# Block 1's neighbourhood attention: stacked Q, compact K, and P·V with V as the stationary operand

## The chip, the core and the metric

The kernel runs on one core of one Trainium2 chip. The metric is device microseconds (us) of one execution; lower is better. TensorE (PE) does matmuls and transposes, and the profile lists its weight loads apart (PEld); DVE, ACT and POOL are the vector, scalar and GpSimd engines, SP issues most DMAs. Each engine runs its own instructions in the order of the program.

## What is computed

Two transformer blocks follow each other on 512 tokens (plus 16 meta tokens in the first). The change lies in the first block's mixer: 8 heads of neighbourhood attention, head width 64, on an 8 x 64 grid. With 8 rows each query sees all 8 rows and 16 columns, plus the 16 meta keys; the meta queries attend to the meta keys alone. Then a root-mean-square norm over all 512 channels, with a gain.

```python
s_loc = jnp.einsum('bhrcd,bhrikd->bhrcik', qg, k_rows) + bias
s_loc = jnp.where(in_win[:, None, :], s_loc, -jnp.inf)
s_meta = jnp.einsum('bhrcd,bmhd->bhrcm', qg, km)
s_all = jnp.concatenate([s_loc.reshape(B, H, R, W, kh * W), s_meta], axis=-1)
p = jax.nn.softmax(s_all, axis=-1)
og = einsum('bhrcik,bhrikd->bhrcd', p_loc, v_rows) + einsum('bhrcm,bmhd->bhrcd', p_meta, vm)
...
o_na = rmsnorm(o_na, na_gain)
mix = jnp.concatenate([o_na, o_gl], axis=-1) @ w_o
```

Beside it the block has a gated linear attention (GLA, 4 heads, both directions), whose work is interleaved with the neighbourhood attention.

## The kernel before

Activations are held channel-major: 128 channels on the partitions, tokens along the row. A weight tile is split into a high and a low part (`wh`, `wl`, type fp32r) by ACT and DVE, so is the activation, and three products replace one (`gemm_outer`, L269 to L286). All projections of block 1 (`ps_w_in`, L284) go through it: each group of 128 output channels is 24 products of 272 tokens and 24 of 256, then a callback takes the result out of PSUM.

The neighbourhood attention goes by pairs of heads p = 0 to 3 (one 128-channel tile is two heads, e = 0, 1). For a pair, `cb_na` takes Q, K and V. Queries are cut into four column tiles `ct` of 16 columns x 8 rows = 128 queries; each sees 32 columns x 8 rows = 256 keys. Q is written into `QW` by column tile; K and V are written four times, once for each tile's 32 columns, by `window` (L551 to L560: eight DVE operations each for K and V), with the 16 meta keys behind (272 columns). V is then transposed (`pvw`, L588) to `VW`.

`na_pair` (L595) has, for each column tile and head (8 units a pair, 32 in all): one score product with 64 rows in type f32 (L615), a DVE operation that adds the mask and bias and finds the row's extreme (L620), the exponential with its sum on ACT (L621), a reciprocal (L622), three transposes of the probabilities (L623 to L625), copies out of PSUM (`pTs` on DVE, `pTm` on ACT), two P·V products with 128 keys and one with the 16 meta keys (L632, L634; the transposed probabilities are the stationary operand, 64 columns of V move), and an ACT copy scaled by the reciprocal (L635) to `ON`, token-major.

After the last pair, `ON` is squared and summed on ACT (L718), the root is taken (L719), each tile is scaled on DVE (L723), transposed back (`pnt`, L726) and split into `mixn`. Then comes `w_o`, whose first half of the products (`part(..., 1, ...)`, six groups of 12 products) needs only GLA's output `mixg`.

The order of the program is made by a scheduler from priorities: GLA first, then `na_pair` (low 1), then the projections (low 2), then `w_ple_2` (low 3) as filler at the end. A score tile takes one of three PSUM banks (`pn_`). Each engine keeps the order that was fixed at build time, whatever is ready.

Of the kernel before, what the change touches and what calls it, by code (L numbers as in the profile page):

```python
# [19 lines left out]
T = NM + S  # L20
# [62 lines left out]
def _pack_w(w, groups, kchunks, rows=None):  # L83
# [3 lines left out]
    for cols in groups:  # L87
# [10 lines left out]
        ("norm_ffn_2", 8), ("norm_ple_2", 8)]  # L98
# [58 lines left out]
class Ker:  # L157
# [130 lines left out]
    def rstd_fin(self, acc, n, pool, pp, name, r=None, rc=None):  # L288
# [14 lines left out]
        nc.scalar.activation(rc, ps[:bs, :nb], AF.Sqrt, bias=self.eps[:bs])  # L303
# [10 lines left out]
    def block1(self, emit):  # L314
# [77 lines left out]
        def cb_gla(gi, si, ps):  # L392
# [14 lines left out]
            elif gi in (3, 4):  # L407
                if si == 0:
                    cur["v"] = gl.tile([128, T], F32, tag="vT", name=f"vT{f}", bufs=2)
# [10 lines left out]
            else:  # L420
                if si == 0:
                    cur["v"] = gl.tile([128, T], F32, tag="vT", name=f"gT{f}", bufs=2)
# [10 lines left out]
        def gla(p):  # L433
# [22 lines left out]
            for d in range(2):  # L456
# [6 lines left out]
                E = gl.tile([128, T], F32, tag="E", name=f"E{p}{d}")  # L463
                iE = gl.tile([128, T], F32, tag="iE", name=f"iE{p}{d}")
# [7 lines left out]
                nc.vector.tensor_tensor(QS[d], qg[p], E, ALU.mult)  # L472
                nc.vector.tensor_tensor(KI[d], kg[p], iE, ALU.mult)
                nc.scalar.activation(DEC[:, d, 1:9], Ex[:, :, last], AF.Copy)
                nc.scalar.activation(DEC[:, d, 0:1], E[:, mlast:mlast + 1], AF.Copy)
                kx, ki = [t[d][:, 16:].rearrange("p (c t) -> p c t", t=64) for t in (KE, KI)]
# [72 lines left out]
        VM = [na.tile([16, 128], F32, name=f"VM{p}", bufs=1) for p in range(4)]  # L549

        def window(dst, ps, si, tagm):  # L551
            iv_ = ps[:, 16:272] if si == 0 else ps[:, 0:256]
            rv_ = rs[:, 16 + 256 * si:272 + 256 * si]
            for ct, w0 in enumerate((0, 8, 24, 32)):
                iv, rv = [t.rearrange("p (r c) -> p r c", c=64)[:, :, w0:w0 + 32] for t in (iv_, rv_)]
                ov = dst[:, ct, 128 * si:128 * si + 128].rearrange("p (r c) -> p r c", c=32)
                nc.vector.tensor_tensor(ov, iv, rv, ALU.mult)
            if si == 0:
                nc.vector.tensor_tensor(tagm, ps[:, 0:16], rs[:, :16], ALU.mult)
                nc.gpsimd.tensor_copy(dst[:, :, 256:272], tagm.rearrange("p (o k) -> p o k", o=1).to_broadcast([128, 4, 16]))  # L560

        def cb_na(gi, si, ps):
            p, j = (gi - 13) // 3, (gi - 13) % 3
            if j == 0:
                if si == 0:
                    cur["Q"] = na.tile([128, 4, 128], F32, tag="QW", name=f"QW{p}")
                    nc.vector.tensor_tensor(QM[:, p, :], ps[:, 0:16], rsq[:, :16], ALU.mult)
                iv = (ps[:, 16:272] if si == 0 else ps[:, 0:256]).rearrange("p (r t c) -> p r t c", r=4, t=4)
                rv = rsq[:, 16 + 256 * si:272 + 256 * si].rearrange("p (r t c) -> p r t c", r=4, t=4)
                base = cur["Q"][:, 0, 127 - 64 * si:128 - 64 * si]  # L570
                ov = bass.AP(base.tensor, base.offset, [list(base.ap[0]), [-16, 4], [128, 4], [-1, 16]])
                nc.vector.tensor_tensor(ov, iv, rv, ALU.mult)
            elif j == 1:
                if si == 0:
                    cur["K"] = na.tile([128, 4, 272], F32, tag="KW", name=f"KW{p}")
                window(cur["K"], ps, si, KM[:, p, :])
            else:
                if si == 0:
                    cur["V"] = na.tile([128, 4, 272], F32, tag="VTW", name=f"VTW{p}", bufs=1)
                    cur["vm"] = na.tile([128, 16], F32, tag="vtm", name=f"vtm{p}")  # L580
                window(cur["V"], ps, si, cur["vm"])
                if si == 1:
# [8 lines left out]
                    nc.tensor.transpose(pm[:16, :128], cur["vm"], ident)  # L591
                    nc.scalar.activation(VM[p], pm[:16, :128], AF.Copy)
                    cur[p] = (cur["Q"], cur["K"], VW)

        def na_pair(p):  # L595
            QW, KW, VW = cur[p]
            sm = na.tile([128, 2, 4], F32, tag="sm", name=f"sm{p}")
            bms = [[], []]
            for t, s in enumerate((15, 7, -1)):
                for e in range(2):  # L600
                    h = 2 * p + e
                    rt = na.tile([128, 256], F32, tag="rpb", name=f"rpb{h}{t}", bufs=2)
# [4 lines left out]
                    nc.gpsimd.tensor_tensor(bm[:, :256], nm[:, t, :256], rt, ALU.subtract)  # L607
                    nc.gpsimd.memset(bm[:, 256:], 0.0)
                    bms[e].append(bm)
            for ct in range(4):  # L610
                pzs = []
                for e in range(2):
                    rr = slice(64 * e, 64 * e + 64)
                    pz = pn_.tile([128, 512], F32, tag="n", name=f"pS{p}{ct}{e}")
                    nc.tensor.matmul(pz[:, :272], QW[rr, ct, :], KW[rr, ct, :], start=True, stop=True)  # L615
                    pzs.append(pz)
                for e, pz in enumerate(pzs):
                    s = na.tile([128, 272], F32, tag="s", name=f"s{p}{ct}{e}", bufs=3)
                    mx = na.tile([128, 1], F32, tag="mx", name=f"mx{p}{ct}{e}", bufs=4)
                    nc.vector.tensor_tensor_reduce(s, pz[:, :272], bms[e][(0, 1, 1, 2)[ct]], 1.0, 1e38, ALU.add, ALU.min, mx)  # L620
                    nc.scalar.activation(s, s, AF.Exp, bias=mx, scale=-1.0, accum_out=sm[:, e, ct:ct + 1])  # L621
                    nc.vector.reciprocal(sm[:, e, ct:ct + 1], sm[:, e, ct:ct + 1])  # L622
                    nc.tensor.transpose(pz[:, 0:128], s[:, 0:128], ident)  # L623
                    nc.tensor.transpose(pz[:, 128:256], s[:, 128:256], ident)
                    nc.tensor.transpose(pz[:16, 272:400], s[:, 256:272], ident)  # L625
                    pT = na.tile([128, 256], F32, tag="pT", name=f"pTs{p}{ct}{e}", bufs=2)
                    pTm = na.tile([16, 128], F32, tag="pTm", name=f"pTm{p}{ct}{e}", bufs=2)
                    nc.vector.tensor_copy(pT, pz[:, :256])
                    nc.scalar.activation(pTm, pz[:16, 272:400], AF.Copy)
# [56 lines left out]
        gr = na2.tile([128, 512], F32, name="na_gain")  # L686
        nc.sync.dma_start(gr, ins["na_gain"].to_broadcast([128, 512]))
# [18 lines left out]
        ptms = na2.tile([16, 8, 16], F32, name="ptms")  # L706
        nc.vector.tensor_copy(ptms, ptm[:16])
        pom = ps_.tile([128, 8, 64], F32, tag="s", name="pom")
        for h in range(8):
            nc.tensor.matmul(pom[:16, h, :], ptms[:, h, :], VM[h // 2][:, 64 * (h % 2):64 * (h % 2) + 64], start=True, stop=True)  # L710
        nc.vector.tensor_tensor(ONm.rearrange("p (h d) -> p h d", h=8), pom[:16], msum.to_broadcast([16, 8, 64]), ALU.mult)

        ss = na2.tile([128, 5], F32, name="nss")
        nc.vector.memset(ss, 1.0)
# [879 lines left out]
```

## Time and profile before

| | us |
|---|---|
| time, median of 3 runs | 1883.17 |
| lowest and highest run | 1872.4, 1884.64 |
| span of the profiled execution | 1873.3 |
| stretch from the first projection to `w_o` (27 to 335 us) in it | 308 |
| PE, DVE, ACT, POOL busy in that stretch | 301.8, 155.2, 132.4, 21.7 |

"Busy" of PE holds the drain of each product, so it overstates how full PE is; the chain of work that ended last, which gives the time from one step to the next, is the better measure. "PEclk" is the granted TensorE clock as a share of its higher level: 1.00 is 2.4 GHz, 0.50 is 1.2 GHz.

### The profile page before, as it was taken

What the parts mean: (1) busy time and instruction counts of PE and PEld (TensorE: products, weight loads), DVE (VectorE), ACT (ScalarE), POOL (GpSimd) and SP (SyncE); (2) the same over time, 40 slices, a digit from 0 to 9 for tenths busy, and PEclk for the clock granted to TensorE, in tenths of its full rate; (3) what the DMA queues carried; (4) which work ended last, traced back from release to release, by engine and by line L of the source; (5) the groups of instructions that cost most, each with busy time, mean ns of one, the idle gap of its engine ahead of it and who ended that gap; (6) DMA issues with size and microseconds to landing.
All of it is one profiled execution on the core that took longest, in us unless ns stands there. A gap on an engine that the chain in (4) does not pass through costs nothing.

```text
span 1873.3 us, 31022 instructions
## 1 busy us (share of the span) xinstructions
PE 1799.5 (96%) x11936; PEld 1506.6 (80%) x11936; DVE 1075.4 (57%) x2274; ACT 770.5 (41%) x1563; POOL 192.2 (10%) x217
## 2 busy tenths in 40 slices
PE   8999999989999999888789989999999999999998
PEld 7788888889998999866566768886678888888887
DVE  5644544787752677866746592437656553255445
ACT  6452434665442445653133432235434442234333
POOL 1000110110000001452211121112000000000000
PEclk9989989999999999998699997589999999999999
DMA  6111121653333334531221113112055333333334
GB/s 189 40 46 46 53 78 57 179 154 111 94 90 96 91 93 136 172 103 46 62 74 48 53 52 81 29 42 86 28 159 161 107 96 96 96 95 92 96 96 130
DMA packets 130789, 171.08 MB, mean 91 GB/s; under 512 B 44455, under 2 KB 59055, under 8 KB 130640
## 3 DMA queue, kind: packets, MB, share of 16 engines
q1 hardware_dynamic: 130640, 169.09, 31.1%
q8 instruction: 94, 1.54, 0.3%
q14 instruction: 55, 0.45, 0.1%
HBM read 155.42 MB, written 13.63 MB: 90 GB/s over the span
## 4 chain that ended last, share of the span: by engine, by line
PE 86%; DVE 7%; DMA 3%; issue 2%; ACT 2%; POOL 0%; SPq 0%; DVEq 0%; ACTq 0%; POOLq 0%
PE ps_w_ff L251 19%; PE ps_w_ffn_in L251 13%; PE ps_w_in L284 7%; PE ps_w_in L251 6%; PE ps_w_ffn_out L251 5%; PE ps_qkv L1277 3%; PE ps_w_out L251 2%; PE ps_w_ple_gate L251 2%; PE pP L1090 2%; PE ps_w_up_rwkv L251 1%; PE py L1214 1%; PE ps_w_up_attn L251 1%; PE ps_first L364 1%; PE paS L1350 1%; PE pS L632 1%
## 5 line engine op out<-in xcount | busy, mean ns | idle before, releaser
L203 DVE TENSOR_TENSOR wl_w_ff<-raw_w_ff,wh_w_ff 128x512 fp32r<-128x512 f32 x128 | 88.2, 689 | 131.6 <-ACT wh_w_ff L202 131.5
L202 ACT ACTIVATE wh_w_ff<-raw_w_ff 128x512 fp32r<-128x512 f32 x128 | 80.9, 632 | 194.7 <-PE ps_w_ff L251 185.9
L202 ACT ACTIVATE wh_w_in<-raw_w_in 128x512 fp32r<-128x512 f32 (+1 forms) x118 | 72.9, 623 | 101.9 <-PE ps_w_in L284 53.0
L203 POOL TENSOR_TENSOR wl_w_in<-raw_w_in,wh_w_in 128x512 fp32r<-128x512 f32 x60 | 82.0, 1371 | 254.6 <-ACT wh_w_in L202 192.2
L202 ACT ACTIVATE wh_w_ffn_in<-raw_w_ffn_in 128x512 fp32r<-128x512 f32 x96 | 60.1, 630 | 100.8 <-PE ps_w_ffn_in L251 87.4
L251 PE MATMUL ps_w_ff<-Yl,wh_w_ff 128*128 128x512 f32 x256 | 101.0, 395 | 0.0
L251 PE MATMUL ps_w_ff<-Yh,wh_w_ff 128*128 128x512 f32 x256 | 101.0, 395 | 0.0
L251 PE MATMUL ps_w_ff<-Yh,wl_w_ff 128*128 128x512 f32 x256 | 101.0, 395 | 0.0
L251 PE MATMUL ps_w_ffn_out<-Y_hi,wl_w_ffn_out 128*128 128x256 f32 (+1 forms) x256 | 83.5, 326 | 2.2 <-DVE wl_w_ffn_out L203 2.1
L251 PE MATMUL ps_w_ffn_out<-Y_hi,wh_w_ffn_out 128*128 128x256 f32 (+1 forms) x256 | 83.7, 327 | 0.0
L251 PE MATMUL ps_w_ffn_out<-Y_lo,wh_w_ffn_out 128*128 128x256 f32 (+1 forms) x256 | 83.5, 326 | 0.0
L251 PE MATMUL ps_w_ffn_in<-fa_hi,wl_w_ffn_in 128*128 128x258 f32 x352 | 73.9, 284 | 3.2 <-DVE wl_w_ffn_in L203 3.2
L203 DVE TENSOR_TENSOR wl_w_ffn_in<-raw_w_ffn_in,wh_w_ffn_in 128x512 fp32r<-128x512 f32 x96 | 65.8, 690 | 19.1 <-ACT wh_w_ffn_in L202 17.9
L251 PE MATMUL ps_w_ffn_in<-fa_hi,wh_w_ffn_in 128*128 128x258 f32 x352 | 73.8, 283 | 1.8 <-ACT wh_w_ffn_in L202 1.8
L203 DVE TENSOR_TENSOR wl_w_ffn_out<-raw_w_ffn_out,wh_w_ffn_out 128x512 fp32r<-128x512 f32 (+1 forms) x72 | 47.8, 669 | 47.7 <-ACT wh_w_ffn_out L202 47.5
L251 PE MATMUL ps_w_ffn_in<-fb_hi,wh_w_ffn_in 128*128 128x258 f32 x352 | 73.8, 284 | 0.0
L251 PE MATMUL ps_w_ffn_in<-fb_hi,wl_w_ffn_in 128*128 128x258 f32 x352 | 73.6, 283 | 0.2 <-DVE wl_w_ffn_in L203 0.2
L251 PE MATMUL ps_w_ffn_in<-fa_lo,wh_w_ffn_in 128*128 128x258 f32 x352 | 73.8, 283 | 0.0
L251 PE MATMUL ps_w_ffn_in<-fb_lo,wh_w_ffn_in 128*128 128x258 f32 x352 | 73.7, 283 | 0.0
L202 ACT ACTIVATE wh_w_ffn_out<-raw_w_ffn_out 128x512 fp32r<-128x512 f32 (+1 forms) x72 | 41.5, 582 | 62.4 <-PE ps_w_ffn_out L251 43.3
L251 PEld LDWEIGHTS ps_w_ffn_in<-fa_hi,wl_w_ffn_in 128*128 128x128 f32 x352 | 55.9, 190 | 3.6 <-DVE wl_w_ffn_in L203 3.6
L251 PEld LDWEIGHTS ps_w_ffn_in<-fa_hi,wh_w_ffn_in 128*128 128x128 f32 x352 | 55.8, 189 | 2.3 <-ACT wh_w_ffn_in L202 2.0
(645 smaller groups left out, 5274.4 us busy)
## 6 DMA issues: line engine op xcount, KB each, us to landing
raw_w_ff<-in_w_ff SPq DMA_DIRECT2D x128, 256.0 KB
raw_w_in<-in_w_in SPq DMA_DIRECT2D x116, 256.0 KB
raw_w_ffn_in<-in_w_ffn_in SPq DMA_DIRECT2D x96, 256.0 KB
raw_w_ffn_out<-in_w_ffn_out SPq DMA_DIRECT2D x40, 256.0 KB
raw_w_o<-in_w_o SPq DMA_DIRECT2D x32, 256.0 KB
raw_w_ffn_out<-in_w_ffn_out SPq DMA_DIRECT2D x32, 192.0 KB
gtd<-gt SPq DMA_DIRECT2D x16, 256.0 KB
g<-gtd SPq DMA_DIRECT2D x16, 256.0 KB
```

The lines of the kernel that those rows point to most:

```text
L202: a = nc.scalar.activation(hi, src, AF.Copy)
L203: v = (eng or nc.vector).tensor_tensor(lo, src, hi, ALU.subtract)
L251: mm = nc.tensor.matmul(ps[si][:ncol, :s1 - s0], a[:, k, :], bk[:, s0:s1], start=(ks == k0 and k == 0 and pi == 0), stop=(ks + k == kend - ...
L284: nc.tensor.matmul(ps[:ncol, :s1 - s0], a[:, k, :], bk[:, s0:s1], start=(n == 0), stop=(n == 3 * kn - 1))
L364: nc.tensor.matmul(p[:ncol, :s1 - s0], a[:, k % 4, :], b[h][:, k % 4, s0:s1], start=(k == 0 and n == 0), stop=(k == 7 and n == 2))
L632: nc.tensor.matmul(po, pT[:, 128 * b:128 * b + 128], VW[:, 2 * ct + b, 64 * e:64 * e + 64], start=(b == 0), stop=False)
L1090: nc.tensor.matmul(pp[:, i, :], BK[rr, 4 * hf + i, :], Z[hf][rr, i, :], start=True, stop=True)
L1214: nc.tensor.matmul(py[H[e], d, :], M[e][:, d, cd[d], 64:128], VU[:, cd[d], H[e]], start=s == 0, stop=True)
L1277: nc.tensor.matmul(pq[i][:, :256], l, r[:, k - ks, :], start=(k == 0 and n == 0), stop=(k == 7 and n == 2))
L1350: nc.tensor.matmul(pS[:, :128 * nk], qT[rr, j, 128 * n:128 * n + 128], kT[rr, 128 * b0:128 * b1], start=True, stop=True)
```

## The change

- **Q** is staged as it is (`stage`), then written to `QS` for each head: 64 partitions hold the high part (ACT), the other 64 the low part (DVE), type fp32r, already cut by column tile.
- **K** is staged with a meta row above and below (10 rows of 64 columns = 640) and written once to `KS`: for each head its high part on both halves of the partitions (ACT, DVE), and its low part on both (POOL, DVE). No copy by column tile: a product reads 9 rows x 32 columns with a stride.
- **Score**: two fp32r products with 128 rows and 288 columns accumulate, in place of one f32 product with 64 rows and 272 columns.
- **P·V**: the probabilities are scaled before the transpose (a DVE `tensor_scalar`, new); V is the stationary operand. Two column tiles are done together: one product with the meta keys of both heads (256 columns), then eight with 64 output channels and 128 moving columns, the two heads by turns on the two halves of the output. `ON` is channel-major and is copied once for two tiles.
- **Norm**: squares are added over the four channel tiles (ACT, DVE), summed by a product with ones (`rstd_fin`), and the scaled result is split to `mixn` by a strided read; no transposes but for the meta tokens.
- `rpb` has one buffer in place of two, `st` tiles replace `vT`, `E` and `iE` share buffers with `QS`, `KI` of GLA.

```diff
-                cur["Q"] = na.tile([128, 4, 128], F32, tag="QW", name=f"QW{p}")
...
+                    cur["QS"] = qs = na.tile([128, 2, 4, 128], F32R, tag="QS", name=f"QS{p}", bufs=1)
+                    qv = qs.rearrange("p e t (r c) -> p e t r c", c=16)
+                    for e in range(2):
+                        nc.scalar.activation(qv[own[e], e], tiles(e), AF.Copy)
+                    for e in range(2):
+                        nc.vector.tensor_tensor(qv[own[1 - e], e], tiles(e), qv[own[e], e], ALU.subtract)
...
-                window(cur["K"], ps, si, KM[:, p, :])
+                stage(st[:, 64:576], ps, si, rs)
...
+                    cur["KS"] = ks = na.tile([128, 2, 2, 640], F32R, tag="KS", name=f"KS{p}", bufs=1)
+                    for e in range(2):
+                        nc.scalar.activation(ks[own[e], e, 0], st[own[e]], AF.Copy)
+                        nc.vector.tensor_copy(ks[own[1 - e], e, 0], st[own[e]])
+                    for e in range(2):
+                        nc.gpsimd.tensor_tensor(ks[own[e], e, 1], st[own[e]], ks[own[e], e, 0], ALU.subtract)
+                        nc.vector.tensor_tensor(ks[own[1 - e], e, 1], st[own[e]], ks[own[e], e, 0], ALU.subtract)
...
-                    rt = na.tile([128, 256], F32, tag="rpb", name=f"rpb{h}{t}", bufs=2)
+                    rt = na.tile([128, 256], F32, tag="rpb", name=f"rpb{h}{t}", bufs=1)
...
-                    nc.tensor.matmul(pz[:, :272], QW[rr, ct, :], KW[rr, ct, :], start=True, stop=True)
+                    for x in range(2):
+                        kv = KS[:, e, x, :].rearrange("p (r c) -> p r c", c=64)[:, r0:r0 + 9, w0:w0 + 32]
+                        nc.tensor.matmul(pz[:, :288].rearrange("p (r c) -> p r c", c=32), QS[:, e, ct, :], kv, start=x == 0, stop=x == 1)
...
                     nc.vector.reciprocal(sm[:, e, ct:ct + 1], sm[:, e, ct:ct + 1])
+                    nc.vector.tensor_scalar(s, s, sm[:, e, ct:ct + 1], None, ALU.mult)
...
-                    po = pz[:, 400:464]
                     for b in range(2):
-                        nc.tensor.matmul(po, pT[:, 128 * b:128 * b + 128], VW[:, 2 * ct + b, 64 * e:64 * e + 64],
-                                         start=(b == 0), stop=False)
-                    nc.tensor.matmul(po, pTm, VM[p][:, 64 * e:64 * e + 64], start=False, stop=True)
-                    nc.scalar.activation(ON[:, ct, 128 * p + 64 * e:128 * p + 64 * e + 64], po, AF.Copy, scale=sm[:, e, ct:ct + 1])
...
+                nc.tensor.matmul(po[:, :256], VMz[p], ptm[:, half], start=True, stop=False)
+                for c in range(2):
+                    for b in range(2):
+                        for e in range(2):
+                            nc.tensor.matmul(po[own[e], 128 * c:128 * c + 128], VW[:, 2 * (ct - 1 + c) + b, own[e]], PT[:, e, c, 128 * b:128 * b + 128],
+                                             start=False, stop=c == 1 and b == 1)
+                nc.scalar.activation(ON[:, p, half], po[:, :256], AF.Copy)
...
+            nc.scalar.activation(sq, ON[:, p, :], AF.Square)
+            if p:
+                nc.vector.tensor_tensor(nacc, nacc, sq, ALU.add)
+        self.rstd_fin(nacc, 512, None, ps_, "rsn", rn, scale=2.0)
...
+            nc.vector.scalar_tensor_tensor(o2, ON[:, p, :], self.v("na_out_gain", p), rn, ALU.mult, ALU.mult)
+            hv, lv = [t[:, p, 16:].rearrange("p (r t c) -> p r t c", r=8, t=4) for t in mixn]
+            self.split(hv, lv, grid(o2))
```

What the scheduler makes of it on PE is shown at the third pair. Before, PE's order from the first P·V products of that pair (`pS` is a score tile, `pTs` and `pTm` are transposed probabilities, `ps_w_in` the next projection):

```order
L632 MATMUL pS_2949<-VW_2900,pTs_2975 128x64 x2
L284 MATMUL ps_w_in_0_3103<-ua_hi,wh_w_in_3093 128x272
L284 MATMUL ps_w_in_0_3103<-ua_lo,wh_w_in_3093 128x272
L634 MATMUL pS_2947<-VM_408,pTm_2960 128x64
L634 MATMUL pS_2949<-VM_408,pTm_2976 128x64
...
L615 MATMUL pS_2985<-KW_2790,QW_2724 128x272
L632 MATMUL pS_2983<-VW_2900,pTs_2995 128x64 x2
L634 MATMUL pS_2983<-VM_408,pTm_2996 128x64
L615 MATMUL pS_3019<-KW_2790,QW_2724 128x272
```

And now, at the same place (`po_na` is the output tile of two column tiles):

```order
L658 MATMUL po_na_3019<-PTM,VMz_408 128x256
L662 MATMUL po_na_3019<-pT_2962,VW_2914 64x128 x8
L642 MATMUL pS_3031<-KS_2832,QS_2757 128x288 x2
L642 MATMUL pS_3045<-KS_2832,QS_2757 128x288 x2
L642 MATMUL pS_3059<-KS_2832,QS_2757 128x288 x2
L284 MATMUL ps_w_in_0_3110<-ua_hi,wl_w_in_3101 128x272
```

The products of a unit no longer come one unit at a time between the projections: nine P·V products stand together, the scores of the next three units behind them, and eleven projection products separate these from the next transposes. PE's order where the first scores of that pair start, between the products of V's projection, is now:

```order
L642 MATMUL pS_2963<-KS_2832,QS_2757 128x288
L284 MATMUL ps_w_in_0_2853<-ub_hi,wl_w_in_2850 128x272
L284 MATMUL ps_w_in_0_2853<-ub_hi,wh_w_in_2849 128x272
L642 MATMUL pS_2977<-KS_2832,QS_2757 128x288
L642 MATMUL pS_2991<-KS_2832,QS_2757 128x288
...
L642 MATMUL pS_2963<-KS_2832,QS_2757 128x288
L642 MATMUL pS_2991<-KS_2832,QS_2757 128x288
...
L642 MATMUL pS_2977<-KS_2832,QS_2757 128x288
```

The first product of each unit (high part of K) stands after 14 to 16 products of V's projection, the second (low part, which POOL and DVE make) after 19 to 23 of them; before, the first score stood after 4. On ACT, in the last pair, the root for the meta tokens is now taken before the last four exponentials:

```order
L664 ACTIVATE ON<-po_na_3426 128x256
L765 ACT_TABLE_LOAD
L765 ACTIVATE nss<-nss,eps 16x1
L646 ACT_TABLE_LOAD
L646 ACTIVATE s_3441,sm_3338<-s_3441,mx_3442 128x272
```

So two table loads stand ahead of `s_3441`, the first exponential of the last pair's second half; before, one stood behind the last of them.

## Rows read from the trace of the kernel before

**Rows 1.** The page: span, and busy time of each engine.

```profile
span 1873.3 us, 31022 instructions
PE 1799.5 (96%) x11936; PEld 1506.6 (80%) x11936; DVE 1075.4 (57%) x2274; ACT 770.5 (41%) x1563; POOL 192.2 (10%) x217
```

**Rows 2.** Busy time by stretch; PEclk is the granted clock, DMA its share.

```profile
core 0: us, PE busy (x) PEld busy (x) DVE busy (x) ACT busy (x) POOL busy (x), PEclk, DMA share, GB/s
82.00:113.00 31.00, 30.86 (x189) 22.73 (x188) 12.93 (x48) 11.15 (x38) 2.67 (x8) 0.78 0.11 27
113.00:204.00 91.00, 90.60 (x685) 75.67 (x685) 48.96 (x139) 37.09 (x101) 2.83 (x9) 0.98 0.19 53
204.00:226.00 22.00, 21.39 (x144) 17.61 (x144) 10.28 (x38) 11.21 (x34) 3.29 (x9) 1.00 0.19 49
257.00:288.00 31.00, 30.75 (x140) 26.58 (x141) 8.71 (x31) 9.28 (x30) 3.02 (x8) 0.61 0.12 30
288.00:335.00 47.00, 44.71 (x279) 34.79 (x278) 23.11 (x75) 26.47 (x74) 2.03 (x6) 0.96 0.26 80
27.00:335.00 308.00, 301.75 (x2078) 248.87 (x2078) 155.18 (x471) 132.41 (x366) 21.71 (x61) 0.93 0.22 61
```

**Rows 3.** Chain that ended last: start, us, engine, tile, line, instructions (f32 product: two).

```profile
35.73 5.82 PE ps_w_in L284 x48
...
87.30 0.22 PE po L520 x2
87.52 0.59 PE po L525 x8
88.11 0.64 PE pa L515 x4
...
280.74 7.32 PE ps_w_in L284 x38
...
304.54 1.10 PE pS L632 x8
...
306.26 0.58 PE pS L634 x4
...
308.16 0.59 PE pS L632 x4
308.74 0.36 PE pS L634 x2
309.10 1.13 PE pS L615 x4
```

**Rows 4.** The same chain from the last P·V product into `w_o`.

```profile
321.55 1.39 PE ps_w_ple L251 x6
...
323.57 0.36 PE pS L634 x2
...
335.07 17.56 PE ps_w_o L266 x144
```

**Rows 5.** Groups by line and shape, 27 to 340 us: busy us, mean ns.

```profile
L620 DVE CUSTOM_DVE_ANT_0 s<-pS,bm 128x272 f32<-128x272 f32 x32 | 13.9, 439 | 23.4 <-PE pS L615 23.3
L622 DVE RECIPROCAL sm<-sm 128x1 f32<-128x1 f32 x32 | 4.9, 157 | 3.6 <-ACT s L621 3.5
L450 DVE TENSOR_TENSOR la<-la,lat 128x256 f32<-128x256 f32 x8 | 2.9, 421 | 2.8 <-ACT lat L448 2.8
L723 DVE SCALAR_TENSOR_TENSOR no<-ON,nss,na_gain 128x512 f32<-128x512 f32 x4 | 2.9, 747 | 0.0
L621 ACT ACTIVATE s<-s,mx 128x272 f32<-128x272 f32 x32 | 16.5, 516 | 16.1 <-DVE mx L620 16.1
L718 ACT ACTIVATE nj<-ON 128x512 f32<-128x512 f32 x4 | 2.5, 622 | 0.1
L719 ACT ACT_TABLE_LOAD x1 | 1.3, 1283 | 0.0
L607 POOL TENSOR_TENSOR bm<-cst,rpb 128x256 f32<-128x256 f32 x24 | 18.2, 757 | 83.8 <-issue 42.4 <-DVE mx L620 23.3 <-DVE sm L622 9.8
```

More of the change, by code (lines that the diff above doesn't have):

```diff
@@ L548, in block1 @@
         KM = na.tile([128, 4, 16], F32, name="KM", bufs=1)
[L549 to L560, printed above, removed]
+        VMz = [na.tile([128, 128], F32, name=f"VMz{p}", bufs=1) for p in range(4)]
@@ L562, in cb_na, with stage @@
+        ptm = na.tile([128, 512], F32, name="PTM", bufs=1)
+        for t in VMz + [ptm]:
+            nc.gpsimd.memset(t, 0.0)
+        own = [slice(0, 64), slice(64, 128)]
+        def stage(dst, ps, si, r):
+            nc.vector.tensor_tensor(dst[:, 256 * si:256 * si + 256], ps[:, 16:272] if si == 0 else ps[:, 0:256], r[:, 16 + 256 * si:272 + 256 * si], ALU.mult)
         def cb_na(gi, si, ps):
             p, j = (gi - 13) // 3, (gi - 13) % 3
+            if si == 0:
+                cur["st"] = na.tile([128, 640], F32, tag="st", name=f"st{p}{j}")
+            st = cur["st"]
@@ L582, in cb_na @@
+                for ct, w0 in enumerate((0, 8, 24, 32)):
+                    iv, rv = [t.rearrange("p (r c) -> p r c", c=64)[:, :, w0:w0 + 32] for t in (iv_, rv_)]
+                    nc.vector.tensor_tensor(cur["V"][:, ct, 128 * si:128 * si + 128].rearrange("p (r c) -> p r c", c=32), iv, rv, ALU.mult)
                 if si == 1:
@@ L705, in block1 @@
             nc.tensor.transpose(ptm[:16, h, :], pmq[:, h, :], ident[:16, :16])
[L706 to L711, printed above, removed]
@@ new lines, in block1 @@
+        ptms = na2.tile([128, 8, 16], F32, name="ptms")
+        for e in range(2):
+            nc.vector.tensor_copy(ptms[64 * e:64 * e + 16, e:8:2], ptm[:16, e:8:2])
+        for e in range(2):
+            pom = ps_.tile([128, 4, 64], F32, tag="s", name=f"pom{e}")
+            for p in range(4):
+                nc.tensor.matmul(pom[:16, p, :], ptms[64 * e:64 * e + 16, 2 * p + e, :], VMz[p][64 * e:64 * e + 16, own[e]], start=True, stop=True)
+            nc.vector.tensor_tensor(ONm.rearrange("q (p e d) -> q p e d", e=2, d=64)[:, :, e], pom[:16], msum[:, e:8:2].to_broadcast([16, 4, 64]), ALU.mult)
@@ new lines, in block1, with grid @@
+        rn = na2.tile([128, 512], F32, name="nrs")
+        nacc = na2.tile([128, 512], F32, name="nacc")
+        for p in range(4):
+            sq = na2.tile([128, 512], F32, tag="no2", name=f"nsq{p}", bufs=2) if p else nacc
+            nc.scalar.activation(sq, ON[:, p, :], AF.Square)
+            if p:
+                nc.vector.tensor_tensor(nacc, nacc, sq, ALU.add)
+        self.rstd_fin(nacc, 512, None, ps_, "rsn", rn, scale=2.0)
+        def grid(t):
+            b = t[:, 127:128]
+            return bass.AP(b.tensor, b.offset, [list(b.ap[0]), [-16, 8], [128, 4], [-1, 16]])
@@ new lines, in block1 @@
+        for p in range(4):
+            o2 = na2.tile([128, 512], F32, tag="no2", name=f"no2{p}", bufs=2)
+            nc.vector.scalar_tensor_tensor(o2, ON[:, p, :], self.v("na_out_gain", p), rn, ALU.mult, ALU.mult)
+            hv, lv = [t[:, p, 16:].rearrange("p (r t c) -> p r t c", r=8, t=4) for t in mixn]
+            self.split(hv, lv, grid(o2))
+        ss = na2.tile([16, 1], F32, name="nss")
+        jk = na2.tile([16, 512], F32, name="nj")
+        nc.scalar.activation(jk, ONm, AF.Square, accum_out=ss)
@@ L734, in block1 @@
+        nc.scalar.activation(ss, ss, AF.Sqrt, bias=self.eps[:16], scale=1.0 / 512)
+        nc.vector.reciprocal(ss, ss)
+        nc.vector.scalar_tensor_tensor(jk, ONm, ss, gr, ALU.mult, ALU.mult)
+        pt = ps_.tile([128, 4, 128], F32, tag="s", name="pnt")
+        for f in range(4):
+            nc.tensor.transpose(pt[:, f, :16], jk[:, 128 * f:128 * f + 128], ident[:16, :16])
+        self.split(mixn[0][:, :, :16], mixn[1][:, :, :16], pt[:, :, :16])
         es2.close()
```

105 lines of the change are left out of this document (47 added, 58 removed).

## The prediction, made before the changed kernel ran

> **What bounds the kernel now.** I read the page first: PE is busy 96% of the span, DVE 57%, ACT 41%, POOL 10% [rows 1]. The change touches only the stretch from 27 us, where the projections start, to 335 us, where `w_o` starts, so I took the busy time by stretch next. There PE is busy 301.8 of 308 us, DVE 155.2, ACT 132.4, POOL 21.7 [rows 2]. The reader should see two things. No other engine is near its limit in any of the four attention stretches (82 to 113, 204 to 226, 257 to 288, 288 to 335 us): DVE is at most at half of its time. And the granted clock is not the same in them: 0.78, 1.00, 0.61, 0.96. What is lost by it is (1 - clock) x length: 6.8, 0, 12.1 and 1.9 us, and 1.8 in the projections from 113 to 204, together 22.6 us [rows 2]. The third view is the chain that ended last, because the time from one PE step to the next is what a step really costs; the mean duration of a product holds its drain. The chain stays on PE nearly throughout, so a microsecond of PE work saved is one off the span, as long as nothing else ends last.
>
> **The scores.** Now 32 f32 products; two of them hold PE 1.13 us [rows 3], 0.565 each, 18.1 us in all. After: 64 fp32r products of 288 columns. The nearest row is `ps_w_in`, 48 products of 272 and 256 columns in 5.82 us [rows 3], 0.121 each for 264 columns, so 0.132 for 288, 8.5 us in all. The term is -9.6 us. The trace has no product that reads its moving operand in runs of 32 columns with a stride; if that halved the rate the term would be 0. I keep -9.6, since the outer stride changes only every 32 columns.
>
> **P·V.** Now a unit costs 0.59 + 0.36 = 0.95 us, and 0.84 in the two units of a pair that go together (1.10 + 0.58 for two) [rows 3]: 2 x 0.84 + 6 x 0.95 = 7.4 us a pair, 29.5 in all. It is dear because a 128x128 stationary operand is loaded for only 64 moving columns. After, each half of a pair has one product with 256 columns, 0.565 x 256/272 = 0.53 us, and eight with 128 columns and 64 output channels. Their price is not in the trace. GLA's products give both ends: four products of 64 rows and 64 outputs in 0.59 us (L525), 0.15 each, two of 64 rows and 128 outputs in 0.64 (L515), 0.32 each; one full product (L520) 0.22 [rows 3]. The new ones alternate between the two halves of the output as L525's do in pairs, so I take 0.20. A half is 0.53 + 1.60 = 2.13 us, eight are 17.0 (13.7 to 24.7). The term is -12.5 us (-15.8 to -4.8).
>
> L525, which switches between parts of the array within four products, costs less per product than L520 [rows 3], so a switch of part has no price that I can see. The Trainium skill, TensorEngine Tiling (Array Packing), Key Properties, says otherwise of the mode itself: changing the tiling mode, not just the tile, drains TensorE. By that rule the new P·V pays two changes per half, 16 in all, but the scores, which leave 64 rows for 128, pay none any more where they paid 32, so the sum would be a little better by the rule and not worse; no run here shows a change of mode by itself, and the sum above goes without it.
>
> **The norm.** From the end of the last P·V product (323.57 + 0.36) to `w_o` (335.07) are 11.1 us [rows 4]. In it stand 28 products of `w_ple_2`, at 1.39/6 = 0.232 us [rows 4] 6.5 us; the other 4.6 are transposes and waits. After, the chain there is: copy 0.45, square 0.62, add at most 0.75, four one-column products about 0.4, table load 1.28 and root about 0.3, reciprocal 0.16, four 128-column products 0.5 [rows 5, 3], and 0.3 for the hand-overs: 4.8 us, with 12 products of `w_ple_2` beside it. The other 16 have moved ahead of the last P·V (3.7 us if they cover nothing). So 11.1 becomes 8.5 or less; I take -3 us. Scaling and splitting (four times 0.75 on DVE plus as many splits, about 7 us) come behind and are hidden: the first 72 of `w_o`'s products need only `mixg`, half of 17.56 us [rows 4]. Without that cover up to 7 us come back.
>
> **The clock.** At the third pair 38 projection products took 7.32 us, 0.193 each against 0.121 [rows 3]: the clock was at its lower level, 1.2 GHz. It fell there after P·V products and 64-row scores, and came back during plain projections; in the second pair, with the same order of products, it did not fall at all (1.00 against 0.61, [rows 2]). So the old mix stands close to a fall and does not always make one. The new mix puts full-height scores and longer-moving P·V products in their place, closer to the projections, in which the clock holds. I take back 10 of the 12.1 us and 2 of the first pair's 6.8, whose GLA products stay as they are: -12 us, between 0 and -22.
>
> **New waits.** A unit's chain gets one DVE operation longer (scaling 272 columns, between the reciprocal's 0.16 and 0.44 as the masked operation takes [rows 5]). Eleven projection products, 1.3 us, stand between the scores and the transposes for it; I count 1 us in all. K is the worse one. From the end of its projection: staging 0.42, ACT copy of 640 columns about 0.75 (0.52 for 272, 0.62 for 512), then POOL's two subtractions one after the other, each at most 0.757 x 640/256 = 1.9 [rows 5]: 5.0 us, while PE's order gives it 23 products and five scores, 23 x 0.121 + 5 x 0.132 = 3.5 us. PE would stand 1.5 us per pair, 0 if POOL's fixed part is large; I count 1, so 4 us in all. Everything queued behind on PE waits with it: V's projection, GLA. The two table loads and the root in the last pair (2.9 us) are covered by 14 products of `w_ple_2` (3.2 us); without these the last exponentials would be late by as much. The extra DVE work (about 6 us a pair: Q and K splits and eight scalings, less the K windows) fits in DVE's idle half. SP's order around the `rpb` loads stays nearly the same, and with one buffer each load waits for POOL's previous subtraction, which is done long before its unit. I count 5 us of waits.
>
> **Sum.** -9.6 - 12.5 - 3 - 12 + 5 = -32 us on the profiled span of 1873.3: 1841. That execution lies beside the fastest run, 1872.4; the median, 1883.17, is 9.9 us above, and the runs are 12.2 us apart, about what one fall of the clock in a pair costs. I add half of 9.9: **1846 us**, and 1834 to 1856 for this case.
>
> **Rivals.**
> - The clock falls as before (for it: the first and the last pair keep GLA and short products; against: fewer of them). Then the 12 us stay: 1858. Chance 0.20.
> - Waits eat the gain: K's low part 3 us late in each pair and each half's chain 2 us late, 28 us where I count 5. For it: four engines hand over within one unit. Against: the order leaves filler at each place. 1846 + 23 = 1869. Chance 0.13.
> - The two heads' P·V products run side by side: two products for L520's 0.22, a half is 0.53 + 0.88 = 1.41 us, 11.3 in all and 5.7 less than my 17.0: 1840. For it L525's price, against it that L525 is not twice as cheap as L520. Chance 0.12. The same page of the Trainium skill, under Key Properties, states that tiles run independently, weight loads and products in parallel.
> - Slower: the clock falls in all four attention stretches and stays low to the end of each, since P·V now fills only half of the array's columns. At half clock 131 us lose 65 in place of 21; with the stretches shortened by 25 us, 37 more than now: 1873.3 - 25 + 5 + 37 = 1890, 1895 beside the median. It decides from 43 us lost (22.6 and the 20 that the work saves). Against it: the trace's fall came with the work that goes. Chance 0.07.
> - My case: 0.48.
>
> **Range and chances.** 1824 to 1868 holds all but the slower case, most of the case with waits, and the best ends of P·V and clock. A measurement of this kernel tells about 1% (19 us) from no change. Faster by more than that means below 1864: my case, side by side, and nearly all of the first rival, 0.78. Within 1%: waits and the rest of the first rival, 0.14. Slower 0.08.
>
> **What would show it.** In the profile after: two scores a unit at about 0.13 us each in the chain; nine P·V products of a half in 1.7 to 2.5 us; the granted clock of the third pair above 0.9; PE's wait for `KS` from POOL below 2 us a pair; `w_o` starting near 303 us instead of 335. A P·V half over 3 us, a clock below 0.8 in two pairs, or waits for `KS` or the scaled `s` above 20 us in sum would make the prediction wrong.

## The result, and the profile after

The changed kernel takes 1852.74 us (median of four runs, 1848.41 to 1853.66) against 1883.91 us beside it: the ratio is 0.9846, interval 0.9816 to 0.9875. It is faster by about 1.5%. In a later comparison, with six runs of it and eleven of the kernel before (median 1876.52), the ratio was 0.9875, interval 0.9833 to 0.9916. One run of a kernel below (P·V only, root late), 2393.19 us at a granted clock of 0.635, stands in that kernel's median and not in its ratio.

The page of the kernel after, to be held against [rows 1]: its span, and busy time of PE, PEld, DVE, ACT and POOL.

```profile
span 1851.3 us, 30948 instructions
PE 1763.1 (95%) x11888; PEld 1481.1 (80%) x11888; DVE 1108.2 (60%) x2311; ACT 780.1 (42%) x1559; POOL 207.6 (11%) x238
```

The span is 22.0 us shorter, PE is busy 36.4 us less, and DVE 33 us more. By stretch, with the columns of [rows 2] (the first row is the whole mixer, up to `w_o`):

```profile
27.00:304.00 277.00, 263.02 (x2045) 219.90 (x2044) 186.61 (x511) 141.73 (x362) 38.41 (x82) 1.00 0.26 70
304.00:309.00 5.00, 4.63 (x26) 4.64 (x27) 3.92 (x7) 2.16 (x5) 0.00 (x0) 0.66 0.19 72
352.00:360.00 8.00, 7.46 (x39) 7.50 (x40) 4.72 (x12) 4.06 (x11) 0.00 (x0) 0.57 0.59 163
382.00:391.00 9.00, 8.39 (x46) 8.39 (x47) 5.49 (x12) 3.78 (x9) 0.00 (x0) 0.62 0.56 168
```

Three things are to be seen. In the whole mixer the granted clock is 1.00, where it was 0.93 [rows 2]. PE stands for 14 of 277 us, where it stood for 6 of 308. And the clock falls three times between the start of `w_o` and 391 us; (1 - clock) x length is 1.7 + 3.4 + 3.4 = 8.5 us there, against 1.7 us between 335 and 420 us in the kernel before.

The chain that ended last, with the columns of [rows 3] (`po_na` is an output tile of P·V, `pS` a score tile):

```profile
199.98 0.70 PE po_na L658 x2
200.68 1.02 PE po_na L662 x16
201.70 1.02 PE pS L642 x6
...
234.12 1.73 DVE KS L591
235.88 2.07 DVE KS L594
...
267.53 2.06 DVE KS L594
269.63 2.07 DVE KS L594
...
283.00 1.28 ACT L765
284.61 1.28 ACT L646
...
292.28 4.31 DMA pled<-ple
296.61 0.61 ACT ple L707
...
304.37 19.12 PE ps_w_o L266 x144
```

A half of P·V (L658 and L662) takes 1.72 us. Six score products take 1.02. `w_o` starts at 304.37 us in place of 335.07, 30.7 us sooner, of which 22.0 are left at the end. Between these rows stand three things that the chain before did not have, or had once (one table load, one copy): K's preparation on DVE, two table loads on ACT, and ACT's copies of `w_ple_2`'s results with their DMA. The longest waits of PE, 27 to 305 us (us in total, times, longest):

```profile
PE pS L642 <- DVE KS L594: 4.2, 4, 1.2
PE ps_w_o L266 <- ACT ple L707: 3.3, 1, 3.3
PE pS L642 <- DVE KS L591: 1.4, 2, 1.1
```

### The profile page after: what moved, and what is told of

Its sections match the earlier page's. It is cut to its first block, busy times and chain, and to the rows that moved or that the text cites. A ratio compares the mean times of both kernels' runs of the same rounds, so it can differ in the third digit from the quotient of the medians.

```text
span 1851.3 us, 30948 instructions
## 1 busy us (share of the span) xinstructions
PE 1763.1 (95%) x11888; PEld 1481.1 (80%) x11888; DVE 1108.2 (60%) x2311; ACT 780.1 (42%) x1559; POOL 207.6 (11%) x238
## 4 chain that ended last, share of the span: by engine, by line
PE 83%; DVE 7%; DMA 4%; issue 3%; ACT 2%; POOL 1%; SPq 0%; DVEq 0%; POOLq 0%; ACTq 0%
PE ps_w_ff L251 19%; PE ps_w_ffn_in L251 13%; PE ps_w_in L284 6%; PE ps_w_in L251 6%; PE ps_w_ffn_out L251 6%; PE ps_qkv L1315 3%; PE ps_w_out L251 2%; PE pP L1128 2%; PE ps_w_ple_gate L251 2%; DMA XH<-scL 1%; PE ps_w_up_attn L251 1%; PE py L1252 1%; PE paS L1388 1%; PE ps_first L364 1%; PE ps_w_o L266 1%
## 5 line engine op out<-in xcount | busy, mean ns | idle before, releaser
L1128 PE MATMUL pP<-Z,BK 64*128 64x128 f32 x256 | 43.7, 354 | 16.7 <-DVE Z L1123 11.4
```

The lines of the kernel that those rows point to most:

```text
L1128: nc.tensor.matmul(pp[:, i, :], BK[rr, 4 * hf + i, :], Z[hf][rr, i, :], start=True, stop=True)
```

## The experiments

One measure goes through all of them: the **stretch**, from 27 us to the start of `w_o`, and the part of it **lost** to the clock, added up from slices of one us as (1 - PEclk) x the slice, as far as PE was busy. Their difference is the stretch at full clock. It differs by up to 2.0 us between profiles of one kernel, and the loss by up to 12.0. Most kernels below have one profile, so a difference under some 2 us at full clock says little.

| kernel | stretch | lost | at full clock |
|---|---|---|---|
| before, three profiles | 308.0, 298.0, 307.6 | 22.2, 10.2, 20.5 | 285.8, 287.8, 287.1 |
| scores only | 294.9 | 8.7 | 286.2 |
| P·V and norm only | 274.8 | 1.7 | 273.1 |
| after, two profiles | 277.4, 279.4 | 0.0, 3.4 | 277.4, 276.0 |
| after, heads apart | 281.8 | 1.7 | 280.1 |
| after, K contiguous | 281.2 | 5.0 | 276.2 |
| after, K's low part on DVE | 276.8 | 5.1 | 271.7 |
| the same, K in halves | 280.0 | 8.5 | 271.5 |
| after, root late | 273.6 | 0.0 | 273.6 |
| P·V only, root late | 277.9 | 6.8 | 271.1 |
| K's low part on DVE, root late | 270.3 | 1.7 | 268.6 |

### The scores alone, and P·V alone

```diff
 # scores only: the kernel before, with Q and K prepared as in the kernel after, and
-nc.tensor.matmul(pz[:, :272], QW[rr, ct, :], KW[rr, ct, :], start=True, stop=True)
+for x in range(2):
+    kv = KS[:, e, x, :].rearrange("p (r c) -> p r c", c=64)[:, r0:r0 + 9, w0:w0 + 32]
+    nc.tensor.matmul(pz[:, :288].rearrange("p (r c) -> p r c", c=32), QS[:, e, ct, :], kv, start=x == 0, stop=x == 1)
 # P.V only: the kernel after, with these lines the other way round, QW and KW written as before
```

> The kernel before with the new scores alone (Q stacked, compact K); P.V, the output layout and the norm stay as before. Stretch from 27 us to w_o before: 308.1 us, of which 22 were lost at the lower clock, so 286 at full clock. Theory P (the old P.V products, short and one unit at a time, bring the clock down): the lower clock stays, 15 to 22 us lost in this stretch; the scores save 8, the waits for K cost 5: stretch 298 to 305, time 1873 to 1885 (between 10 less than the kernel before and no change). Theory S (the scores of half height bring it down): under 4 us lost, stretch 283 to 287, time 1858 to 1865. If falls come by chance, in neither pattern: between.

> The kernel before with the new P.V and the new norm alone; scores, Q and K as before (f32, 64 rows, four windows of K). At full clock 286 us less 15 (P.V) and 2 (norm) is 269; hidden waits of the longer chain add 0 to 5. Theory P: under 4 us lost at the lower clock between 27 us and w_o, stretch 269 to 278, time 1843 to 1853, so as fast as the full change or faster, since the waits for K are gone. Theory S: 15 to 22 us lost, stretch 284 to 296, time 1860 to 1873.

The scores alone: 1869.60 us, ratio 0.9956 (0.9921 to 0.9991), stretch at full clock 286.2, so nothing saved there. The clock took 8.7 us, between the figures of the two theories, and the kernel before lost 10.2 us in one of its profiles (below). P·V and norm alone: 1849.27 us, ratio 0.9868 (0.9809 to 0.9926), 1.7 us lost, at full clock 273.1. That is 3.6 us less than the full change: beside the new P·V, the new scores with their preparation of Q and K cost more than they saved. Theory P is borne out in half: 1.7 us lost with the new P·V, but 8.7 and not 15 to 22 with the old one. One fall can be tied to the old P·V. This is the stretch 94 to 112 us, the first pair's P·V with GLA's products between, in the profile with the scores alone and in that with P·V alone (columns as in [rows 2]):

```profile
94.00:112.00 18.00, 18.00 (x122) 14.75 (x122) 9.04 (x36) 9.59 (x30) 3.08 (x8) 0.81 0.15 30
```

```profile
94.00:112.00 18.00, 17.69 (x141) 13.61 (x142) 11.63 (x39) 9.80 (x27) 2.44 (x8) 1.00 0.17 34
```

The clock is 0.81 there with the old P·V and the new scores, 1.00 with the new P·V and the old scores.

### The kernel before, twice more

> The kernel before once more, unchanged, for a second profile. If its lower clock between 27 and 335 us is a property of the order of products, the same stretches at half clock come again (95 to 109, 262 to 287 us; 20 to 24 us lost). If it falls by chance, other stretches or other lengths, and with them the 12 us between its runs: a time near 1884 would have about 10 us more lost somewhere than the profile at hand.

> The kernel before, a third profile. Two profiles lost 22 and 10 us at the lower clock ahead of the output projection, at 95 to 109 and 135 to 140 us in both, at 262 to 287 us in one alone. If the falls at 95 to 109 us belong to the order of products there and the rest is chance, it falls there again, and somewhere else; the stretch less its loss is 286 to 288 us.

The second profile, of a run of 1861.74 us, and the third, of one of 1871.98 us, each at the first pair, the third pair (as in [rows 2]) and the last:

```profile
94.00:112.00 18.00, 18.00 (x95) 12.45 (x95) 7.14 (x30) 6.68 (x23) 2.44 (x7) 0.72 0.08 16
257.00:288.00 31.00, 30.61 (x226) 25.75 (x225) 14.85 (x54) 11.56 (x39) 4.06 (x11) 1.00 0.15 43
302.00:320.00 18.00, 17.89 (x92) 13.11 (x91) 7.02 (x23) 13.80 (x40) 0.00 (x0) 1.00 0.38 117
```

```profile
94.00:112.00 18.00, 18.00 (x84) 12.19 (x84) 6.98 (x28) 6.72 (x24) 1.66 (x5) 0.62 0.07 16
257.00:288.00 31.00, 30.61 (x213) 26.07 (x211) 12.83 (x48) 11.70 (x36) 3.56 (x10) 0.94 0.18 55
302.00:320.00 18.00, 18.00 (x59) 12.64 (x58) 4.84 (x20) 8.15 (x26) 0.00 (x0) 0.53 0.10 30
```

The third pair's fall, on which my prediction built most (0.61 in [rows 2]), is not there in the second profile and nearly gone in the third, which has another long one at 302 to 320 us. So that place was chance. The fall between 95 and 111 us is in all three profiles and in the one with the scores alone: in four of four with the old P·V, and in none of the ten with the new P·V. These ten lose 0 to 8.5 us elsewhere, 3.4 on the mean; the three of the kernel before lose 17.6 on the mean. One of the ten (P·V only, root late) stood at half clock (0.51) from 71 to 85 us, in the first pair's old scores and GLA's products, before any P·V. What sets off the other falls stays open.

### P·V: the two heads side by side or not

```diff
-for c in range(2):
-    for b in range(2):
-        for e in range(2):
+for e in range(2):
+    for c in range(2):
+        for b in range(2):
             nc.tensor.matmul(po[own[e], 128 * c:128 * c + 128], ...
```

> The changed kernel with the eight P.V products of a half in another order: the four of one head, then the four of the other, so neighbours no longer lie on different halves of the output's columns. In the changed kernel eight take 1.02 us (0.13 each), against 0.22 for one product of full width. If the two heads' products run side by side, the same eight now take about 8 x 0.22 = 1.76 us (0.7 more per half, 6 us in all). If 0.13 is simply the price of a product with 64 outputs, they stay at 1.02.

PE's timeline (start, us, engine, line, operation) at one half of the second pair, first as in the kernel after, then with the heads apart:

```profile
200.61 1.09 PE L662 MATMUL po_na<-pT,VW 128*64 128x128 f32 x16
201.63 1.09 PE L642 MATMUL pS<-KS,QS 128*128 128x288 f32 x6
202.56 0.49 PE L609 MATMUL pvw<-cst,VTW 128*128 128x128 f32 x3
```

```profile
202.24 1.58 PE L662 MATMUL po_na<-pT,VW 128*64 128x128 f32 x16
203.75 1.08 PE L642 MATMUL pS<-KS,QS 128*128 128x288 f32 x6
```

From start to start the eight products take 1.02 us by turns and 1.51 apart, 0.128 and 0.189 each. The trace's starts of the single instructions (two to a product) say more. By turns two start 0.007 us apart, one on each half, and such a pair follows the other every 0.109 us. Apart, the first head's start one by one every 0.109 us, and from its fifth on the second head's come between them. So instructions on different halves of the output's columns do run side by side, two in the time of one. The whole is 1.48 times as quick and not twice, since the heads apart still overlap in the middle and both orders have the same ends: 0.16 us behind the first start or pair, 0.20 behind the last. The stretch at full clock grows by 3 to 4 us, as 8 x 0.49 = 3.9 says. The Trainium skill, TensorEngine Tiling (Array Packing), Key Properties, has different tiles load weights and multiply in parallel; the trace agrees, with its pairs 0.007 us apart.

### The scores' price: the stride is not in it

```diff
-kv = KS[:, e, x, :].rearrange("p (r c) -> p r c", c=64)[:, r0:r0 + 9, w0:w0 + 32]
+kv = KS[:, e, x, :288]
```

> The changed kernel, but each score product reads 288 columns of K that lie side by side (the first 288) in place of 9 runs of 32 with a stride of 64: the scores are those of other keys, the work of PE is the same. In the changed kernel six score products in a row take 1.02 us, 0.17 each, where a projection product of 264 columns takes 0.121, which would be 0.132 for 288. If the stride costs the difference, six now take 0.79 us. If the stationary operand or the type costs it, they stay at 1.02.

The same timeline of this kernel:

```profile
202.95 1.09 PE L642 MATMUL pS<-KS,QS 128*128 128x288 f32 x6
203.88 0.49 PE L609 MATMUL pvw<-cst,VTW 128*128 128x128 f32 x3
```

Six products take 0.93 us from start to start with the stride (201.63 to 202.56, above) and 0.93 without. The stride costs nothing. What lies above the projections' 0.132 stands at the start of a group: by the trace's starts in the kernel after, a score that follows another holds PE 0.136 us (median of 36), one that follows other work 0.22 (mean of 28); without the stride it is 0.133 and 0.22. What makes the first one dear is not shown.

### K's preparation

```diff
-nc.gpsimd.tensor_tensor(ks[own[e], e, 1], st[own[e]], ks[own[e], e, 0], ALU.subtract)
+nc.vector.tensor_tensor(ks[own[e], e, 1], st[own[e]], ks[own[e], e, 0], ALU.subtract)
```

> The changed kernel with K's low part made by DVE alone: four subtractions of 64 x 640 on DVE, none on POOL. In the changed kernel DVE's take 0.82 to 2.07 us each and POOL's 1.5 to 2.0, at the same time. Theory A (the two engines slow each other): alone DVE takes 0.82 each, 3.3 us for four in place of 4.1 for two beside two; PE's waits for K fall from 5.6 us to 2 to 3. Theory B (2.07 is DVE's own price at the third pair): 8 us for four, the waits grow to 15 to 20 us and the time by 10 to 15.

All subtractions by their line (count, then ns: least, median, most; first and last start), in the kernel after and in this one:

```profile
L593 POOL TENSOR_TENSOR KS<-st,KS x8: 1537/1704/2022, 69.8 to 269.0; 64x640 fp32r<-64x640 f32 x8
L594 DVE TENSOR_TENSOR KS<-st,KS x8: 818/1674/2065, 74.2 to 269.6; 64x640 fp32r<-64x640 f32 x8
L591 DVE CAST KS<-st x8: 486/488/1726, 70.1 to 267.0; 64x640 fp32r<-64x640 f32 x8
```

```profile
L593 DVE TENSOR_TENSOR KS<-st,KS x8: 806/821/825, 74.8 to 269.7; 64x640 fp32r<-64x640 f32 x8
L594 DVE TENSOR_TENSOR KS<-st,KS x8: 818/820/1281, 75.8 to 271.0; 64x640 fp32r<-64x640 f32 x8
```

Theory A holds for the price. A subtraction costs DVE 0.82 us by itself (one of sixteen took 1.28) and 2.06 beside POOL's; even DVE's copy went from 0.49 to 1.73. Four on DVE alone take 3.3 us, two beside two of POOL's 4.1. The Trainium skill, SBUF — State Buffer, Who interferes with whom, has a DVE instruction with two inputs in SBUF contend with a GpSimd instruction that reads SBUF. The trace agrees: at the last pair DVE's first subtraction, begun at 267.53 us, ends at 269.59, 0.7 us behind the end of POOL's first (267.05 + 1.87).

PE's waits for `KS` are gone (5.6 us before), and the stretch at full clock falls from 276.7 (mean of two) to 271.7. But the scheduler also gave PE another order. The last product of the last pair's first scores, in the kernel after and in this one:

```profile
271.83 0.37 PE L642 MATMUL pS<-KS,QS 128*128 128x288 f32 x1 [1.09 <-DVE KS L594]
```

```profile
271.89 0.40 PE L642 MATMUL pS<-KS,QS 128*128 128x288 f32 x1
```

In the kernel after it starts 4.70 us behind the first product that reads this K (267.13), with 10 projection products on the way; here 4.30 us behind it (267.59), with 25. K's last subtraction ends at 271.69 and at 271.84. Counted from that first product, K was whole only 0.3 us sooner at this pair, and the wait was mostly filled with other products. What the price alone is worth to the stretch, and what the order, these runs do not separate.

```diff
 # as above, and after each half of K's projection, si = 0 and 1:
+ks, z = cur["KS"], slice(320 * si, 320 * si + 320)
 for e in range(2):
-    nc.scalar.activation(ks[own[e], e, 0], st[own[e]], AF.Copy)
+    nc.scalar.activation(ks[own[e], e, 0, z], st[own[e], z], AF.Copy)
... # the copy and the two subtractions on DVE likewise
```

> As the kernel with K's low part on DVE alone, and the first half of K (rows 0 to 4 with the meta row) is split right after the first half of its projection, beside the 24 products of the second half. Behind the second half only 320 columns are left: by theory A about 0.42 + 0.45 + 4 x 0.45 = 2.7 us, less than PE's 3.5 us of other work in between. PE's waits for K fall below 1 us; the start of the output projection moves from 304.4 to about 299 us if the clock holds. If more than K's preparation stood in the way of the scores' gain, it stays at 302 or later.

One wait of 0.3 us for `KS` is left, and the stretch at full clock is 271.5: nothing more than with DVE alone. Two waits changed against each other: those for V's preparation (`pvw`, `pvwm`) fell from 3.5 to 1.1 us, and a new one of 2.8 us stands ahead of the meta tokens' transposes (`ptm`, released by ACT's `pmq`). So this run does not settle whether halves would pay without the new wait. `w_o` started at 307.0, because this profile lost 8.5 us to the clock.

### The root that came too early

```diff
-nc.scalar.activation(ss, ss, AF.Sqrt, bias=self.eps[:16], scale=1.0 / 512)
+ep = na2.tile([16, 1], F32, name="nep")
+nc.vector.scalar_tensor_tensor(ep, rn[:16, 0:1], 0.0, self.eps[:16], ALU.mult, ALU.add)
+nc.scalar.activation(ss, ss, AF.Sqrt, bias=ep, scale=1.0 / 512)
```

> The changed kernel with the root for the meta tokens behind the norm's own root (its constant is made to depend on the norm's result): the two table loads and the root, 2.9 us of ACT ahead of the last pair's last four exponentials, go. My prediction counted them as covered by 14 products of the filler. If they are, the output projection starts as before at 304 us. If not, ACT's copies of the filler's results come sooner too, PE's wait of 3.3 us for the last of them ends, and the output projection starts 3 to 6 us sooner, at 298 to 301.

The chain at the same place, without the table loads:

```profile
282.40 1.02 PE pS L642 x6
283.42 1.40 PE ps_w_ple L251 x6
284.82 0.27 PE pS L650 x2
...
299.99 0.60 ACT ple L707
...
300.63 4.45 PE ps_w_o L266 x35
```

The transposes follow the scores after 1.4 us of filler, where they came after 3.8 (from 283.41 to 287.17 us): 14 products of filler and a wait of 0.34 us. PE's wait for the last copy of `w_ple_2` shrinks from 3.3 to 1.2 us, and `w_o` starts at 300.6 us. So the filler covered the table loads where they stood. What they held up was ACT's own queue, and with it the copies of `w_ple_2` that `w_o` waits for.

### The best of these together

```diff
-nc.gpsimd.tensor_tensor(ks[own[e], e, 1], st[own[e]], ks[own[e], e, 0], ALU.subtract)
+nc.vector.tensor_tensor(ks[own[e], e, 1], st[own[e]], ks[own[e], e, 0], ALU.subtract)
...
-t = pl.tile([128, S], F32, tag="pe", name=f"ple{k}", bufs=2)
+t = pl.tile([128, S], F32, tag="pe", name=f"ple{k}", bufs=4)
 # and the root late, as above; the second kernel: P.V only, with the last two
```

> The changed kernel with K's low part on DVE alone, the meta tokens' root behind the norm's, and four buffers in place of two for the filler's results on their way to memory. One by one the first two moved the start of the output projection from 277.4 us behind the first projection to 271.7 and 273.6 (clock losses taken out). If these add: 268 or a little less, start at 295 us plus what the clock takes (0 to 9 in the profiles so far), time 10 us below the changed kernel, 1840 to 1846. If they cover each other: 271 or more, at most 6 us below it.

> The new P.V and norm with the old scores, and the same two changes at the end (root late, four buffers). It differs from the kernel with K's low part on DVE in the scores, Q and K alone. The scores' products cost 15.7 us in the old form (64 x 0.246) and 11.8 in the new one (64 x 0.184). If these 4 us are what the new scores are worth once K is in time: 4 us slower than that kernel, 272 less 4 = 268 from the first projection to the output projection here against 264 there. If the new scores are worth nothing: equal within 2 us.

> The changed kernel once more, beside the two others on one chip, with a second profile. If no fall of the clock between 27 us and the output projection is a property of the new order, again under 2 us are lost there. If falls come by chance and are only rarer than before, between 0 and 9 us lost, as in the kernels that differ from it in one detail.

| kernel, same chip | median us | ratio to before, interval |
|---|---|---|
| K's low part on DVE, root late | 1841.52 | 0.9822 (0.9777 to 0.9866) |
| P·V only, root late | 1847.94 | 0.9841 (0.9798 to 0.9884) |
| after | 1852.46 | 0.9875 (0.9833 to 0.9916) |

The first is 11 us below the changed kernel; the intervals overlap, but five of its six runs (1828.23 to 1851.75) lie below the lowest of the other's six (1847.25 to 1860.26), and the stretch at full clock says 8.1 us (276.7 to 268.6), the sum of 5.0 and 3.1 for the two repairs one by one. So they add, as far as one profile of each shows it. The four buffers were not tried alone; PE's wait for the last copy of `w_ple_2` is 1.2 us with four as with two. The changed kernel's second profile lost 3.4 us in its mixer, in falls at 164 and 239 us, so the 0.0 of the first is not a property of its order. The page of the first kernel, and its mixer and the 123 us behind it:

```profile
span 1826.5 us, 30939 instructions
```

```profile
27.00:297.00 270.00, 261.98 (x2031) 219.79 (x2030) 180.56 (x511) 136.25 (x355) 26.05 (x74) 0.99 0.25 70
297.00:420.00 123.00, 114.38 (x936) 111.83 (x937) 100.93 (x187) 77.51 (x158) 14.04 (x16) 1.00 0.52 150
```

This profile is of the fastest of the six runs: behind 420 us the clock took 60 us, against 72 in the first profile of the changed kernel. Against it, P·V alone with the late root is 2.5 us longer at full clock (271.1). This would be what the new scores are worth with K made by DVE alone, but 2.5 us between single profiles is hardly more than two profiles of one kernel differ by, and the times of these two can't be told apart.

## Why the prediction was right, step by step

The time, 1852.74 us, lies in the range of my case (1834 to 1856), and `w_o` started at 304.4 us, where I had said 303. That start is luck: two errors of about ten us stood against each other. Without the clock my sum was -9.6 - 12.5 - 3 + 5 = -20.1 us; between the two profiles the stretch at full clock went from 285.8 to 277.4, -8.4 (by the means of three and two profiles, 286.9 and 276.7, -10.2). The clock gave more than I took: -22.2 between these two profiles in place of -12 (on the mean 17.6 us lost before and 1.7 after, -16). Of the signs that I had named, the third pair's clock (1.00), a half of P·V, PE's waits for `KS` (1.4 us a pair, though DVE's subtractions end them and not POOL's) and the start of `w_o` came out; the scores at 0.13 us did not.

To size the terms I took, in each kernel, PE's time from one start to the next in slices at full clock, less the waits that the timeline names.

- **Scores: the step that failed.** I expected -9.6. The products cost 16.1 to 17.2 us before, by profile, and 11.4 after, -4.7 to -5.8: a new one costs 0.18 and not 0.132 (the projection's price held for a score behind another, 0.136, but 28 of 64 stand first in their group at 0.22, a start that I had put at nothing; the stride I had worried about is not in it), an old one 0.50 to 0.54 and not 0.565. K's waits took it back: with the scores alone PE waited 7.0 us for `KS` and the stretch at full clock did not move (286.2); beside the new P·V the scores made it 3.6 us longer, and with K on DVE they are worth 2.5 us at the most that one pair of profiles shows.
- **P·V: right, a little better.** I expected 29.5 to 17.0 us; it was 27.6 to 13.4, -14.2 in place of -12.5. A half takes 1.6 to 1.7 us, not 2.13. The rival with the two heads side by side was right about the mechanism and, but for the ends of a run, about the price: two products every 0.22 us. My 0.20 for one had them one after the other.
- **Norm: -2.1 in place of -3.** From the last P·V product to `w_o` are 9.0 us (295.33 to 304.37) in place of 11.1 [rows 4], and 3.3 of these are PE's wait for a copy of `w_ple_2`, which I had not seen coming.
- **Waits: +5 expected; the waits that the timeline names grew from 5.9 to 13.8 us.** For K I had 4 and it was 5.6, with the right operand but the wrong engine at its end: I put each of POOL's subtractions at 1.9 (it was 1.5 to 2.0), and did not see that DVE's, which end later, slow down beside them. The table loads were covered by 14 products of filler, as I had said, but not in ACT's queue, which I had left out: without them the stretch at full clock is 3.1 us shorter.
- **Clock: right in sign, about right in size, half right in reason.** I argued from the third pair's fall, which the second profile of the same kernel doesn't have. The fall that goes with the old P·V is the first pair's, of which I had taken back only 2 us.
- **The way from the stretch to the end.** I carried the mixer's gain to the end unchanged, which gave a span of 1841. In the profile 8.7 of the 30.7 us were gone again: 6.8 are the falls behind the start of `w_o`, the other 2 are not placed (from 420 us to the end the granted clock is 0.95 in both). The second profile of the changed kernel lost 1.7 between `w_o` and 420 us, not 8.5, so this too differs from run to run.

PE's steps and waits by this reckoning come to -11 to -13 us, the stretch at full clock to -10.2. Part of the difference is the measure: at the lower clock the steps of the kernel before took a little less than twice as long, so that the loss is put 1 to 2.5 us too high in its profiles. Of the other rivals, the clock falling as before and the clock low to the end of all four stretches are out: 0 and 3.4 us lost. The slower one was also mispriced: 131 us less the 21 lost and the 25 saved are 85 us of work at full clock, which would lose 85 at half of it, 64 more than before and not 37. The waits did eat into the gain, with 8 us and not 28.

## What to carry to other kernels

Price a product with its neighbours: a price from a long run of projections held inside a run of scores, but each start of a run cost 0.09 us more, and the new scores came out a quarter too low. Before two engines share the preparation of one operand, compare what each takes alone with what both take together, and where a scheduler makes the order, see whether it moved the products too before a gain is put down to the price. Look for instructions of a late stage that a scheduler may bring forward to where they change another engine's tables. Where a clock's falls decide over ten microseconds, one profile of the kernel before is not enough to say which of them belong to the code.

## What the runs showed that I had not expected

- DVE beside POOL: 0.82 us became 2.06 for a subtraction of 64 x 640, 0.49 became 1.73 for a copy, so that two engines took longer (4.1 us) than one (3.3).
- The clock's falls in the mixer are largely chance: the same kernel lost 22.2, 10.2 and 20.5 us, at partly other places. Its second and third profiles come from different chips, but thirteen runs on one chip already lie between 1860.66 and 1887.82 us.
- A fall often came when PE had stood just ahead of `w_o`: of the ten profiles with the new P·V, seven have a wait of PE there of 3.3 or 3.8 us, and in six of these the clock fell in the wait itself or right behind it (0.66 from 304 to 309 us in the kernel after). In the three with a wait of 1.2 to 2.2 us it did not. That is no rule: with the scores alone the clock fell there without such a wait. The cause is not shown.
- Two products with 64 output columns on different halves run side by side: a pair of instructions every 0.109 us, as long as a single one takes. The order decides how much: 1.02 us for eight products by turns and 1.51 head by head.
